# Where split weights are kept between chunks, and a new order at the start of a two-layer trunk

## The chip, the cores and the metric

The kernel runs on one NeuronCore of one Trainium2 chip. The metric is the device time in microseconds (us) of one execution, as the median of several runs. Beside the timed runs stands one profiled execution, from which every instruction's start and duration is known. In its rows PE is TensorE (PEld its weight loads), DVE is VectorE, ACT is ScalarE, POOL is GpSimd, and SP is SyncE, whose queue issues nearly all DMAs in order. A small q (SPq) marks an engine's sequencer.

## The reference, cut to what matters

The input x has 2048 tokens of 1024 channels. Layer A is a pooling mixer, layer B an attention whose weights are products of "keep" factors along the keys. Each layer ends with a gated embedding term.

```python
def rms_norm(x, g):
    return (x * lax.rsqrt(jnp.mean(x * x, axis=-1, keepdims=True) + EPS)) * g
...
for i in range(2):                                   # layer 0 is A, layer 1 is B
    if i == 0:                                       # A: pooling mixer
        h = rms_norm(x, a_norm[0])
        u, z = split(h @ w_in)                       # 1024 -> 2 x 1024
        pooled = trailing_mean(u, (2, 4, 8, 16)) - u # four groups of 256 channels
        mixed = einsum(pooled, w_group) * scale      # one 256 x 256 map a group
        x = x + (mixed * silu(z)) @ w_out
    else:                                            # B: stick-breaking attention
        k, v = split(rms_norm(x, kv_norm) @ w_kv)    # 16 heads of 64
        q, z = split(rms_norm(x, b_norm[0]) @ w_in)
        o = stick_breaking_attention(rms_norm(q), rms_norm(k), v)
        x = x + (o * silu(z)) @ w_out
    x = x + (p[i] @ ple_w[i]) * sigmoid(x @ ple_gate_w[i])
```

All of it is in float32.

## The kernel before

**Splitting.** A matrix operand is held as a pair: a high part, which is the number rounded to the type that TensorE takes at full rate (`float32r`), and a low part, the rest. A product of two pairs takes three matmuls: high by high, high by low, low by high. So each 128 x 512 piece of a weight, 0.26 MB as float32, becomes a pair of 0.52 MB. `put_split` (L145) makes it: one instruction on ACT rounds, one on POOL or DVE subtracts. Where a norm's gain belongs to the weight, ACT and DVE multiply by it on the way (L153, L154); where none does, two subtractions in three go to POOL and one to DVE (L147, L149).

**The plan of weights.** The list `plan` (L220 to L241) names every weight unit in the order in which TensorE takes it. `pump` (L179) loads units ahead of use, as many as `UNITS` = 9 weight tiles allow; a tile is given back (L191) when its last matmul is written. A unit with `keep` set is stored to scratch memory in HBM as a pair when it has been split (L169), and the next time its key comes up the pair is loaded as it is (L161). A unit without it is loaded raw (L164) into one of four `io` tiles, and split each time. The `io` tiles also serve the residual `xr`, the embedding input and the next chunk's x. Before, z of A (`za`), z of B (`zb`), and q, k, v are kept; the output weights `ao`, the gate `ag` and the embedding weights `al` of layer A are not.

**Stages.** The tokens are cut into four chunks of 512. For each chunk, `first_part` runs the mixer, the output projection (`out_steps`), the gate (`gate_steps`), z of B (`gate_z`), and q, k, v for the first eight heads (`kvq`, b = 0). `second_part` runs q, k, v for the other eight (b = 1). In chunk 0 each group's u weights are first multiplied with the group's map on the chip (`fold`), and the results kept as `wf`. A last pass, `post`, runs the output projection and gate of layer B for each chunk.

**Two streams on TensorE.** Chunk 0's first part runs alone, with six PSUM banks for dense products. From then on attention is written out slot by slot (L912 to L934), a slot being one head and one block of 512 keys, and `fill` puts a share of the dense stream's matmuls between the parts of each slot. There the dense products have two PSUM banks. `fill` also calls `keep` (L759) every 36 steps once the first half of chunk 1 is done: it loads one unit of layer B's output or gate weights, splits it, and stores it, 36 units in all.

**Order.** The order on each engine is chosen by a scheduler from the order written and its own estimate of times. With `state["hold"]` set, matmuls stay in the order written (L52); with `state["boot"]` set, so do the instructions passed through `booted`. At the start, `boot` (L395) loads the first weights and x, folds group 3 and computes the tokens' mean squares on TensorE (`sum_first`, L384): eight squares on ACT, and for each four products with a column of ones, which are two instructions each.

Of the kernel before, what the change touches and what calls it, by code (L numbers as in the profile page):

```python
# [11 lines left out]
AF = mybir.ActivationFunctionType  # L12
# [3 lines left out]
P = 128  # L16
D = 1024
S = 2048
KT = D // P
# [17 lines left out]
def trunk_kernel(ctx, tc, x, p, a_norm, wu_t, wz_a, w_group, a_scale, a_w_out, kv_norm, w_kv,  # L37
# [73 lines left out]
    def bank(tag, nm):  # L111
        return psum.tile([P, W5], F32, tag=tag, name=nm)
# [7 lines left out]
    def turned():  # L120
        return bank("psa", "pst").rearrange("q (j t) -> q j t", j=4)
# [7 lines left out]
    def booted(ins):  # L129
        if state["boot"]:  # L130
            tc.keep_in_program_order(ins)
# [47 lines left out]
    def pump():  # L179
        while wq["out"] < len(plan) and wq["out"] - wq["back"] < wq["cap"]:  # L180
            key, src, kts, n, gain, keep = plan[wq["out"]]
            if src is None and (key not in once or wq["out"] < first_chunk):
                return
            held.append(unit(key, src, kts, n, gain, keep))
            wq["out"] += 1

    def take(n):
        pump()
        return [held.popleft() for _ in range(n)]
# [7 lines left out]
    def plan_block(nm, src, b, gain=None, keep=False, order=PAIRS):  # L197
        for kts in order:
            plan.append(((nm, b, kts), None if src is None else src[b], kts, WB, gain, keep))

    def plan_wide(nm, src, b, gain):
        for kt in range(KT):
            plan.append(((nm, b, kt), src[b], (kt,), W5, gain, True))

    def plan_kvq(b):
        plan_wide("q", b_w_q, b, g_b)
        plan_wide("k", w_kv, b, g_kv)
        plan_wide("v", w_kv, 2 + b, g_kv)

    def plan_group(g):  # L210
        plan.append((("wg", g), w_group[g], (0, 1), WB, None, False))
# [8 lines left out]
    for s in range(NSUB):  # L220
        for g in (3, 2, 1, 0):
            if s == 0:
                plan_group(g)
            plan_block("za", wz_a, g, g_a, True)
            plan_block("wf", None, g)
        for b in range(4):
            plan_block("ao", a_w_out, b, order=PAIRS[::-1])
        for b in range(4):
            plan_block("ag", gate_a, b)
            plan_block("al", ple_a, b, order=PAIRS[:1])  # L230
        if s + 1 == NSUB:
            plan_kvq(0)
        for b in range(4):
            plan_block("zb", b_w_z, b, g_b, True)
        if s + 1 < NSUB:
            plan_kvq(0)
        plan_kvq(1)
        if s == 0:
            first_chunk = len(plan)
    for c in range(NSUB):  # L240
# [83 lines left out]
    def bcast(r, nm):  # L324
        ps = turned()
        for j in range(4):
            T.transpose(ps[:, j, :], r[:, j : j + 1].to_broadcast([P, P]), ident)
        rb = pool.tile([P, W5], F32, tag="rb", name="rb" + nm, bufs=2)
        A.copy(out=rb, in_=ps.rearrange("q j t -> q (j t)"))
        return rb  # L330
# [7 lines left out]
    def rooted(ps, nm):  # L338
        ss = pool.tile([P, 4], F32, tag="ss" + nm, name="ss")
        A.copy(out=ss, in_=ps[:, 0, 0:4])  # L340
        r = pool.tile([P, 4], F32, tag="r" + nm, name="r")
        rsqrt_mean(r, ss, D, nm)
        return r
# [14 lines left out]
    def load_first():  # L358
        two = [t4("u0") for _ in range(2)]
        for h in range(2):  # L360
            for c in range(2):
                first_u[c, h] = f(two[h])[:, c]
                ins = (nc.scalar if c else nc.sync).dma_start(out=first_u[c, h],
                                                             in_=wu_t[6 + c, :, h * W5 : (h + 1) * W5])
                if not c:
                    booted(ins)
            if h == 0:
                pump()
        nc.scalar.dma_start(out=g_a, in_=a_norm)
        for o in range(KT):  # L370
            xin = (qryt, ppt, keyt, valt)[(0, 2, 0, 3, 0, 2, 0, 3)[o]]("xin", F32)
            ins = (nc.scalar if o == 1 else nc.sync).dma_start(out=xin, in_=x[o * P : (o + 1) * P, 0:W5])
            if o != 1:
                booted(ins)
            first_x.append(xin)
# [5 lines left out]
            booted((G if o % 2 else V).tensor_tensor(out=pr[:, 1], in0=first_x[o], in1=f(pr[:, 0]), op=ALU.subtract))  # L381
            chunk[0].setdefault("x", []).append(pr)

    def sum_first():  # L384
        sums = turned()
        for i in range(KT):
            sq = tmp("sq")
            booted(A.activation(out=sq, in_=first_x[i], func=AF.Square))
            for j in range(4):
                tc.keep_in_program_order(  # L390
                    T.matmul(sums[:, 0, j : j + 1], sq[:, j * P : (j + 1) * P], ones,
                             start=(i + j == 0), stop=(i == KT - 1 and j == 3)))
        chunk[0]["rb1"] = bcast(rooted(sums, "x"), "x")

    def boot():  # L395
        load_first()
        later.pop(0)()
        fold_split(3, first_u)
        wq["cap"] = UNITS
        pump()  # L400
        run = fold(3)

        def folds(n):
            for _ in range(n):
                next(run, None)

        cast_first(range(4))
        folds(13)
        cast_first(range(4, KT))
        folds(12)  # L410
        later.pop(0)()
        folds(12)
        later.pop(0)()
        later.pop(0)()
        folds(12)
        later.pop(0)()
        sum_first()
        while later:
            later.pop(0)()
        for dst, v in ((g_s, a_scale), (g_b, b_norm), (g_kv, kv_norm), (gs[:, 0:1], k_norm), (gs[:, 1:2], b_q_norm)):  # L420
            nc.sync.dma_start(out=dst, in_=v)
        booted(V.scalar_tensor_tensor(out=gqk, in0=gs[:, 1:2], scalar=HD ** -0.5, in1=gs[:, 0:1],
                                      op0=ALU.mult, op1=ALU.mult))
        state["boot"] = False
        pump()

    def prep(s):
        ck = chunk[s]
# [23 lines left out]
    def pooled(s, o, ps, zr):  # L452
# [22 lines left out]
        split(pr, po, G if o > 1 else V)  # L475
        ck["m"][o] = pr

    def mixer(s):
        ck = chunk[s]
        ck["m"] = {}  # L480
        for g in (3, 2, 1, 0):
            if s == 0 and g < 3:
                yield from fold(g)
            us, zs = take(4), []
            for k in range(2):
                ps = dense()
                yield from product(ps, us, ck["x"], k * P, k)
                zs.append(silu(ps, ck["rb1"]))
            if s == 0 and g:
                fold_load(g - 1)  # L490
            us = take(4)
            for k in range(2):
                ps = dense()
                yield from product(ps, us, ck["x"], k * P, k)
                pooled(s, 2 * g + k, ps, zs[k])
# [405 lines left out]
    def fill(share):  # L901
        nonlocal owed, count
        owed += share
        while owed >= 1.0:
            next(run, None)
            owed -= 1.0
            count += 1
            if count % 36 == 0 and kept and (1, 0) in marks:
                keep(*kept.pop(0))

    scan = None
# [92 lines left out]
```

## Time and profile before

| | us |
|---|---|
| median of 3 runs (2810.36 to 2812.27) | 2812.25 |
| the profiled execution | 2817.46 |
| its span, first to last instruction | 2815.7 |
| PE busy | 2733.7 |
| DVE busy | 1847.9 |
| ACT busy | 1272.0 |
| POOL busy | 863.9 |

The DMA queues moved 643.37 MB at a mean of 228 GB/s over the span. The mean granted clock of TensorE was 0.985 of full.

How to read the rows that follow. A row of the waits gives who waited for whom, the total in us, how often, and the longest. A row of the busy times by stretch starts with the stretch in us from the span's start and its length, then each engine's busy time with the number of instructions in brackets (PE, PEld, DVE, ACT, POOL), then TensorE's granted clock, the share of the time in which the DMA engines were busy, and the GB/s that they moved. A row of the timeline gives start, duration, engine, line, operation, output and inputs, shape, the count of instructions merged into it, and in square brackets the idle time before it and what ended that. A row for one line or tile gives the count, the shortest, median and longest duration in ns, and the first and last start in us.

### The profile page before, as it was taken

The numbers are of one execution on the slowest core, as the hardware profiler recorded it, in microseconds if no ns is written. First come the engines' busy times: TensorE is split into PE (matmuls) and PEld (weight loads), VectorE is DVE, ScalarE is ACT, GpSimd is POOL, SyncE is SP. The second block draws the span as 40 slices with busy tenths as digits, with TensorE's granted clock in tenths as the row PEclk, the third lists the DMA queues.
The fourth block names the chain that finished last, engine by engine and source line by source line (L and its number), as shares of the span: only waits on it lengthen the run. The fifth ranks groups of instructions, "written<-read, shape, count | busy, mean of one in ns | idle before, by whom it ended". The sixth has DMA issues, their size and how long they took to land.

```text
span 2815.7 us, 38145 instructions
## 1 busy us (share of the span) xinstructions
PE 2733.7 (97%) x13400; PEld 2249.9 (80%) x13400; DVE 1847.9 (66%) x2373; ACT 1272.0 (45%) x2496; POOL 863.9 (31%) x695
## 2 busy tenths in 40 slices
PE   8999979999989999999999999999999999999999
PEld 7888857878867887788778888888888888888777
DVE  5745445755434786765558889777777877777872
ACT  5335543344334345544444456554554444444441
POOL 2354422445432354554222334221211101111002
PEclk9999989999999999999999999999999999999999
DMA  6648899556788966787785544778587767656545
GB/s 236 213 148 291 300 321 317 185 173 216 255 276 277 335 225 211 239 305 234 246 272 183 153 143 155 256 221 266 178 253 228 241 212 251 216 193 227 180 125 186
DMA packets 306123, 643.37 MB, mean 228 GB/s; under 512 B 48646, under 2 KB 81414, under 8 KB 305932
## 3 DMA queue, kind: packets, MB, share of 16 engines
q1 hardware_dynamic: 305356, 640.16, 68.9%
q8 instruction: 105, 1.72, 0.3%
q14 instruction: 86, 0.70, 0.1%
q10 hardware_dynamic: 576, 0.79, 0.1%
HBM read 471.43 MB, written 161.02 MB: 225 GB/s over the span
## 4 chain that ended last, share of the span: by engine, by line
PE 77%; DMA 9%; DVE 6%; issue 2%; SPq 2%; POOL 2%; ACT 2%; ACTq 0%; DVEq 0%; POOLq 0%
PE psd L46 53%; PE pso L46 8%; PE psl L46 8%; PE psa L50 7%; DMA wpair<-once 2%; DVE pp L815 2%; DMA vs<-vr 2%; DVE at L832 1%; DMA wraw<-in_gate_a_dram 1%; PE pst L50 1%; DMA wraw<-in_w_kv_dram 1%; DVE wpair L154 1%; DMA wraw<-in_b_w_q_dram 1%; PE pst L46 1%; SPq L595 0%
## 5 line engine op out<-in xcount | busy, mean ns | idle before, releaser
L815 DVE TENSOR_TENSOR_SCAN pp<-pp,floor 128x512 f32<-128x512 f32 (+3 forms) x640 | 777.0, 1214 | 26.4 <-ACT pp L811 25.5
L832 DVE TENSOR_TENSOR at<-psa,at 128x512 fp32r<-128x512 f32 (+3 forms) x640 | 387.1, 605 | 440.1 <-ACT at L830 437.7
L46 PE MATMUL psd<-wpair,x 128*128 128x512 f32 x2304 | 619.8, 403 | 33.6 <-DMA wpair<-once 17.1
L830 ACT CAST at<-psa 128x512 fp32r<-128x512 f32 (+3 forms) x640 | 333.4, 521 | 668.1 <-PE psa L50 644.5
L46 PE MATMUL psd<-x,wpair 128*128 128x512 f32 x2304 | 600.3, 393 | 2.1 <-ACT sg L546 2.1
L46 PEld LDWEIGHTS psd<-wpair,x 128*128 128x128 f32 x2304 | 427.7, 191 | 132.8 <-DMA wpair<-once 27.8
L46 PEld LDWEIGHTS psd<-x,wpair 128*128 128x128 f32 x2304 | 427.9, 188 | 91.0 <-ACT sg L546 2.8
L46 PE MATMUL psd<-xp,wpair 128*128 128x512 f32 x1536 | 390.0, 395 | 0.4 <-DMA wpair<-once 0.4
L46 PE MATMUL pso<-at,vv 128*128 128x512 f32 (+3 forms) x1280 | 362.4, 364 | 0.2 <-DVE at L832 0.2
L50 PE MATMUL psa<-ident,pp 128*128 128x128 f32 x2176 | 346.8, 274 | 14.2 <-DVE pp L815 5.7
L50 PEld LDWEIGHTS psa<-ident,pp 128*128 128x128 f32 x2176 | 274.6, 140 | 100.9 <-DVE at L832 11.1
L811 ACT ACTIVATE pp<-psl 128x512 f32<-128x512 f32 (+3 forms) x640 | 344.4, 538 | 6.6 <-PE psl L46 3.3
L46 PEld LDWEIGHTS psd<-xp,wpair 128*128 128x128 f32 x1536 | 286.6, 189 | 59.4 <-DMA wpair<-once 0.8
L46 PE MATMUL psl<-kk,qa 128*128 128x512 f32 (+3 forms) x640 | 284.4, 444 | 4.3 <-DMA kk<-kd 3.0
L46 PEld LDWEIGHTS pso<-at,vv 128*128 128x128 f32 x1280 | 241.8, 189 | 54.4 <-DVE at L832 0.5
L46 PE MATMUL psl<-kk,qb 128*128 128x512 f32 (+3 forms) x640 | 234.3, 366 | 0.0
L46 PE MATMUL psd<-mp,wpair 128*128 128x512 f32 x768 | 197.9, 399 | 6.9 <-DVE xr L514 6.9
L46 PE MATMUL psd<-og,wpair 128*128 128x512 f32 x744 | 202.5, 394 | 2.0 <-DVE os L845 2.0
L149 POOL TENSOR_TENSOR wpair<-wraw,wpair 128x512 fp32r<-128x512 f32 x101 | 146.8, 1458 | 138.1 <-ACT wpair L147 136.7
L46 PEld LDWEIGHTS psd<-mp,wpair 128*128 128x128 f32 x768 | 145.4, 192 | 38.1 <-DVE xr L514 7.7
L46 PEld LDWEIGHTS psd<-og,wpair 128*128 128x128 f32 x744 | 137.5, 188 | 31.3 <-DVE os L845 2.6
L539 POOL TENSOR_TENSOR xj<-x 128x512 f32<-128x512 f32 x64 | 101.8, 1594 | 134.2 <-DVE sg L550 127.5
(117 smaller groups left out, 2750.1 us busy)
## 6 DMA issues: line engine op xcount, KB each, us to landing
wpair<-once SPq DMA_DIRECT2D x384, 512.0 KB
once<-wpair SPq DMA_DIRECT2D x80, 512.0 KB
kk<-kd SPq DMA_DIRECT2D x160, 256.0 KB
vv<-vd SPq DMA_DIRECT2D x160, 256.0 KB
wpair<-wf SPq DMA_DIRECT2D x48, 512.0 KB
once<-kp SPq DMA_DIRECT2D x36, 512.0 KB
wraw<-in_a_w_out_dram SPq DMA_DIRECT2D x64, 256.0 KB
wraw<-in_gate_a_dram SPq DMA_DIRECT2D x64, 256.0 KB
```

Of the source, the lines that this page charges most:

```text
L46: return held_in_order(nc.tensor.matmul(*a, **k))
L50: return held_in_order(nc.tensor.transpose(*a, **k))
L149: (G if state["lo"] % 3 else V).tensor_tensor(out=pr[:, 1], in0=raw, in1=f(pr[:, 0]), op=ALU.subtract)
L154: booted(V.scalar_tensor_tensor(out=pr[:, 1, i], in0=raw[:, i], scalar=g, in1=f(pr[:, 0, i]), op0=ALU.mult, op1=ALU.subtract))
L539: G.tensor_tensor(out=xj, in0=f(x1[o][:, 0]), in1=f(x1[o][:, 1]), op=ALU.add)
L811: A.activation(out=pp[:, r0:], in_=ps[:, :w], func=AF.Sigmoid, scale=-1.0)
L815: V.tensor_tensor_scan(out=pp[:, r0:][:, ::-1], data0=pp[:, r0:][:, ::-1], data1=least, initial=1.0 if st["diag"] else st["carry"][j], op0 ...
L830: A.copy(out=at[:, 0, cs], in_=pt[:, cs])
L832: return lambda: V.tensor_tensor(out=at[:, 1, cs], in0=pt[:, cs], in1=f(at[:, 0, cs]), op=ALU.subtract)
```

## The change

It has four parts.

1. The units of q, k and v for the second eight heads (b = 1) are not stored in chunk 0. They are loaded raw again in chunk 1, split and stored there, and loaded as pairs in chunks 2 and 3.
2. The units of `ao`, `ag` and `al` (16, 16 and 4 a chunk) are stored as pairs in chunk 0 and loaded as pairs in chunks 1 to 3.
3. The start: matmuls are held in the written order from the first one on. Three matmuls of the identity with a constant tile, whose result nobody reads, are written ahead of the first fold. Then z's two products of group 3 come first, with the sums of the squares written between the matmuls of the second, then u's two products, with the norm's broadcast and z's SiLU written into the first. The loads of group 2's u weights are written behind them.
4. `keep` starts when the second half of chunk 1 is done, and runs every 54 steps in place of 36.

```diff
--- before.py
+++ after.py
@@ -198,14 +198,15 @@
         for kts in order:
             plan.append(((nm, b, kts), None if src is None else src[b], kts, WB, gain, keep))
 
-    def plan_wide(nm, src, b, gain):
+    def plan_wide(nm, src, b, gain, keep):
         for kt in range(KT):
-            plan.append(((nm, b, kt), src[b], (kt,), W5, gain, True))
-
-    def plan_kvq(b):
-        plan_wide("q", b_w_q, b, g_b)
-        plan_wide("k", w_kv, b, g_kv)
-        plan_wide("v", w_kv, 2 + b, g_kv)
+            plan.append(((nm, b, kt), src[b], (kt,), W5, gain, keep))
+
+    def plan_kvq(s, b):
+        keep = s >= b
+        plan_wide("q", b_w_q, b, g_b, keep)
+        plan_wide("k", w_kv, b, g_kv, keep)
+        plan_wide("v", w_kv, 2 + b, g_kv, keep)
 
     def plan_group(g):
         plan.append((("wg", g), w_group[g], (0, 1), WB, None, False))
@@ -224,17 +225,17 @@
             plan_block("za", wz_a, g, g_a, True)
             plan_block("wf", None, g)
         for b in range(4):
-            plan_block("ao", a_w_out, b, order=PAIRS[::-1])
+            plan_block("ao", a_w_out, b, keep=True, order=PAIRS[::-1])
         for b in range(4):
-            plan_block("ag", gate_a, b)
-            plan_block("al", ple_a, b, order=PAIRS[:1])
+            plan_block("ag", gate_a, b, keep=True)
+            plan_block("al", ple_a, b, keep=True, order=PAIRS[:1])
         if s + 1 == NSUB:
-            plan_kvq(0)
+            plan_kvq(s, 0)
         for b in range(4):
             plan_block("zb", b_w_z, b, g_b, True)
         if s + 1 < NSUB:
-            plan_kvq(0)
-        plan_kvq(1)
+            plan_kvq(s, 0)
+        plan_kvq(s, 1)
         if s == 0:
             first_chunk = len(plan)
     for c in range(NSUB):
@@ -381,19 +382,27 @@
             booted((G if o % 2 else V).tensor_tensor(out=pr[:, 1], in0=first_x[o], in1=f(pr[:, 0]), op=ALU.subtract))
             chunk[0].setdefault("x", []).append(pr)
 
-    def sum_first():
-        sums = turned()
-        for i in range(KT):
-            sq = tmp("sq")
-            booted(A.activation(out=sq, in_=first_x[i], func=AF.Square))
-            for j in range(4):
-                tc.keep_in_program_order(
-                    T.matmul(sums[:, 0, j : j + 1], sq[:, j * P : (j + 1) * P], ones,
-                             start=(i + j == 0), stop=(i == KT - 1 and j == 3)))
-        chunk[0]["rb1"] = bcast(rooted(sums, "x"), "x")
+    def square_first(i):
+        if i == 0:
+            chunk[0]["sums"] = turned()
+        sq = tmp("sq")
+        booted(A.activation(out=sq, in_=first_x[i], func=AF.Square))
+        for j in range(4):
+            T.matmul(chunk[0]["sums"][:, 0, j : j + 1], sq[:, j * P : (j + 1) * P], ones,
+                     start=(i + j == 0), stop=(i == KT - 1 and j == 3))
+
+    def norm_first():
+        chunk[0]["rb1"] = bcast(rooted(chunk[0].pop("sums"), "x"), "x")
+
+    def warm():
+        ps = bank("pso", "warm")
+        for _ in range(3):
+            T.matmul(ps, ident, floor, start=True, stop=True)
 
     def boot():
+        state["hold"] = True
         load_first()
+        warm()
         later.pop(0)()
         fold_split(3, first_u)
         wq["cap"] = UNITS
@@ -414,15 +423,10 @@
         later.pop(0)()
         folds(12)
         later.pop(0)()
-        sum_first()
-        while later:
-            later.pop(0)()
         for dst, v in ((g_s, a_scale), (g_b, b_norm), (g_kv, kv_norm), (gs[:, 0:1], k_norm), (gs[:, 1:2], b_q_norm)):
             nc.sync.dma_start(out=dst, in_=v)
         booted(V.scalar_tensor_tensor(out=gqk, in0=gs[:, 1:2], scalar=HD ** -0.5, in1=gs[:, 0:1],
                                       op0=ALU.mult, op1=ALU.mult))
-        state["boot"] = False
-        pump()
 
     def prep(s):
         ck = chunk[s]
@@ -475,11 +479,42 @@
         split(pr, po, G if o > 1 else V)
         ck["m"][o] = pr
 
+    def hooked(gen, hooks):
+        for n, _ in enumerate(gen):
+            for h in hooks.get(n, ()):
+                h()
+            yield
+
+    def mixer_first():
+        ck = chunk[0]
+        ck["m"] = {}
+        us = take(4)
+        pss = [dense(), dense()]
+        yield from product(pss[0], us, ck["x"], 0, 0)
+        hooks = {3 * i: [lambda i=i: square_first(i)] for i in range(KT)}
+        yield from hooked(product(pss[1], us, ck["x"], P, 1), hooks)
+        while later:
+            later.pop(0)()
+        us = take(4)
+        zs = []
+        hooks = {8: [norm_first], 9: [lambda: zs.extend(silu(ps, ck["rb1"]) for ps in pss)]}
+        for k in range(2):
+            ps = dense()
+            yield from hooked(product(ps, us, ck["x"], k * P, k), {} if k else hooks)
+            pooled(0, 6 + k, ps, zs[k])
+        state["boot"] = state["hold"] = False
+        fold_load(2)
+        while later:
+            later.pop(0)()
+
     def mixer(s):
         ck = chunk[s]
-        ck["m"] = {}
-        for g in (3, 2, 1, 0):
-            if s == 0 and g < 3:
+        if s == 0:
+            yield from mixer_first()
+        else:
+            ck["m"] = {}
+        for g in (3, 2, 1, 0)[s == 0 :]:
+            if s == 0:
                 yield from fold(g)
             us, zs = take(4), []
             for k in range(2):
@@ -905,7 +940,7 @@
             next(run, None)
             owed -= 1.0
             count += 1
-            if count % 36 == 0 and kept and (1, 0) in marks:
+            if count % 54 == 0 and kept and (1, 1) in marks:
                 keep(*kept.pop(0))
 
     scan = None
```

## The prediction

> **What bounds the kernel now.** I read the page first, then TensorE's waits, then the busy time and clock of each stage of chunk 0, then the instructions around the longest stalls.
>
> ```profile
> span 2815.7 us, 38145 instructions
> PE 2733.7 (97%) x13400; PEld 2249.9 (80%) x13400; DVE 1847.9 (66%) x2373; ACT 1272.0 (45%) x2496; POOL 863.9 (31%) x695
> once<-wpair SPq DMA_DIRECT2D x80, 512.0 KB
> PE psd L46 <- DMA wpair<-once: 17.5, 20, 4.8
> PE psd L46 <- ACT wpair L153: 14.0, 6, 9.3
> PE psd L46 <- ACT uh L293: 7.5, 2, 7.0
> PE psd L46 <- DVE xr L514: 6.9, 2, 4.1
> PE psd L46 <- ACT sg L546: 3.7, 3, 2.1
> PE psd L46 <- DMA wpair<-once: 14.8, 13, 4.8
> ```
>
> TensorE sets the time: it idles 82.0 us of 2815.7 (span less busy), and the change touches no matmul of the steady part. So all it can win is idle time and time at the halved clock. Nearly all named waits are late weights or late operands of dense products (the last line is the same view for 700 to 1000 us alone). The stages of chunk 0 (the columns behind the busy times are granted clock, DMA share, GB/s):
>
> ```profile
> 100.00:136.60 36.60, 36.60 (x186) 31.28 (x185) 24.14 (x40) 12.99 (x24) 16.16 (x16) 1.00 0.61 208
> 136.60:180.10 43.50, 43.50 (x194) 36.03 (x193) 18.46 (x25) 15.04 (x25) 20.31 (x16) 1.00 0.43 136
> 180.10:234.50 54.40, 54.40 (x242) 45.06 (x241) 36.23 (x45) 28.56 (x54) 31.17 (x22) 1.00 0.58 195
> 234.50:279.40 44.90, 44.90 (x206) 37.33 (x205) 21.66 (x33) 21.06 (x42) 17.13 (x14) 1.00 0.88 316
> 279.40:345.00 65.60, 65.60 (x301) 54.17 (x300) 31.48 (x44) 33.96 (x54) 32.00 (x29) 1.00 0.86 308
> 345.00:375.00 30.00, 15.79 (x60) 11.14 (x59) 8.66 (x13) 9.93 (x17) 5.51 (x5) 0.68 0.91 291
> 375.00:400.00 25.00, 23.47 (x98) 17.86 (x97) 11.19 (x17) 10.48 (x18) 7.85 (x9) 0.97 0.99 313
> 400.00:452.00 52.00, 49.03 (x226) 38.73 (x227) 26.68 (x40) 23.51 (x41) 12.47 (x11) 0.97 0.95 322
> 346.33 0.48 SPq L169 DMA_DIRECT2D once<-wpair  x1
> 369.04 0.43 SPq L169 DMA_DIRECT2D once<-wpair  x1
> ```
>
> In order these are the end of the mixer, A's output projection, gate, B's z, the first half's q/k/v, and (345 to 452) the second half's. The last three rows hold 14.2 + 1.5 + 3.0 = 18.7 us of idle TensorE at 291 to 322 GB/s and a DMA share over 0.9: here memory traffic is the bound. Seven stores of split weights are issued from the first to the second of the last two lines. Ahead of it, A's output projection uses 136 GB/s.
>
> **Step B, chunk 0's stores.** The 24 stores of the second half's q/k/v leave chunk 0; 16 + 16 + 4 = 36 stores of A's output, gate and embedding weights enter it. A store is 0.524 MB. Leaving: seven in 345 to 375, 3.67 MB, at that row's 291 GB/s 12.6 us of its 14.2 us idle. The other 17, 8.9 MB, are 36% of the 24.6 MB of the two rows behind, whose idle time of 4.5 us I take to vanish but for 0.5. Entering: 18.9 MB between about 111 and 234. At the 322 GB/s of the busiest row the spare room is 25.6 x 114 = 2.9 MB, 43.5 x 186 = 8.1 and 54.4 x 127 = 6.9, together 17.9 MB: 1.0 MB, or 3.1 us, is late, and the two rows behind have 1.2 MB of room for it. I take 10 us in 345 to 375, 4 us behind it, and 4 us of clock ((1 - clock) x busy gives at most 5.1 + 0.7 + 1.5 = 7.3): **-18**. Best: all 18.7 + 7.3, -26. Worst: the copies sustain only 308, the spare is 25.6 x 100 + 43.5 x 172 + 54.4 x 113 = 16.2 MB, 2.7 MB or 9 us is late and nothing behind absorbs it; with the q/k stores also part of the wait, -6. Each entering store waits at SP's head for its subtraction, and the next raw loads stand behind it; the lookahead of nine weight tiles hides that, and if it is used up, each late microsecond is TensorE's.
>
> A rule of the Trainium skill ("DMA: Bandwidth & Descriptors", Specifications) puts a core's HBM share near 358 GB/s, and its Bandwidth section has a single core alone at up to 425. No row of these stages passes 322 at a share of 0.95. With 358 the estimated lag is zero and B is 3 us better; the rows decide, so I keep 322.
>
> **Step C, output and gate of chunks 1 to 3.** The 36 units a chunk come back as one 0.5 MB load in place of a 0.25 MB load, a copy on ACT and a subtraction on POOL or DVE; 108 of each go. These run beside TensorE, so their busy time is worth nothing by itself. What counts is the four `io` tiles, which raw weights share with the residual `xr`:
>
> ```profile
> 566.00 6.44 SPq L508 DMA_DIRECT2D xr<-in_x_dram  x4
> 569.38 1.30 DVE L514 TENSOR_TENSOR xr<-psd,xr 128x512 f32<-128x512 f32 x2 [1.43 <-DMA xr<-in_x_dram]
> 570.12 4.61 PE L46 MATMUL psd<-mp,wpair 128*128 128x512 f32 x12 [2.78 <-DVE xr L514]
> 1059.81 1.65 PE L46 MATMUL psd<-mp,wpair 128*128 128x512 f32 x3 [4.07 <-DVE xr L514]
> 1618.91 0.47 PE L50 MATMUL psa<-ident,pp 128*128 128x128 f32 x1 [2.04 <-DVE pp L815]
> 550.00:600.00 50.00, 47.22 (x213) 38.30 (x212) 29.77 (x37) 21.38 (x43) 25.51 (x18) 0.97 0.51 162
> 1050.00:1100.00 50.00, 45.93 (x212) 37.69 (x212) 30.95 (x36) 22.91 (x47) 22.25 (x16) 0.93 0.61 200
> ```
>
> `xr` is loaded only behind raw weights, DVE adds it late, and the two PSUM banks hold TensorE. The xr waits are 6.9 us; sg's 3.7 and the 2.0 at 1618.91 stand behind queues that hold splits. The clock costs about 0.03 x 47 + 0.07 x 46 = 4.6 us more in the two stages. Of these 17.2 us I take **-10**: the pair loads too queue on SP ahead of xr, waiting for a weight tile. Bounds -17 (all) and 0 (none). The extra 9.4 MB a chunk go where DMA is at 162 to 200 GB/s.
>
> **Step D, the moved stores and `keep`.** Chunk 1's second half (about 820 to 920 us) now loads 0.25 MB raw, splits it and stores: 24 x 0.26 MB more traffic, 24 x (0.721 + 0.746) us on ACT and DVE. B's output weights, 36 units of 0.79 MB, start only after it, one per 54 steps for 36. Today's take 832.8 to 1226.0, 10.9 us each: about eight fewer lie there, 6.3 MB against 6.3 MB. At 10.9 x 1.5 = 16.4 us each, 36 of them from about 920 then reach to about 1510.
>
> ```profile
> L153 ACT ACTIVATE wpair<-wraw,gains x80: 493/721/728, 217.2 to 429.3; 128x512 fp32r<-128x512 f32 x48, 128x256 fp32r<-128x256 f32 x32
> L154 DVE SCALAR_TENSOR_TENSOR wpair<-wraw,gains,wpair x80: 471/746/1751, 218.1 to 430.0; 128x512 fp32r<-128x512 f32 x48, 128x256 fp32r<-128x256 f32 x32
> L149 POOL TENSOR_TENSOR kp<-kraw,kp x22: 1261/1294/2272, 832.8 to 1226.0; 128x512 fp32r<-128x512 f32 x22
> 800.00:850.00 50.00, 42.89 (x182) 34.19 (x181) 16.56 (x24) 15.60 (x30) 11.69 (x11) 0.90 0.95 304
> 850.00:900.00 50.00, 44.13 (x206) 34.73 (x205) 21.95 (x33) 20.21 (x40) 15.54 (x15) 0.93 0.79 272
> 1450.00:1500.00 50.00, 46.76 (x232) 38.58 (x233) 36.18 (x47) 21.76 (x46) 13.09 (x10) 0.97 0.90 282
> ```
>
> The new wait is the split's: behind ACT's copy stand the attention's sigmoids, behind DVE's subtraction the scans. DVE has room (22 of 50 us), so I take +1 there; bounds: -8 (half the weight bytes it waits for), +8 (half of L153's 14.0 plus clock). Past 1226 a keep per 16.4 us adds 48 GB/s, to 330 where the last row has 282 and idles 3.2 us in 50; the row at 304 idles 7.1. Over the 284 us I take +5, bounds 0 and +12 (three such stretches at 3.9 us more). **+6**.
>
> **Step A, the start.**
>
> ```profile
> 7.02 0.79 PE L46 MATMUL psd<-wpair,uh 128*128 128x256 f32 x2 [7.02 <-ACT uh L293]
> 16.72 12.88 PE L46 MATMUL psd<-xp,wpair 128*128 128x512 f32 x56
> 23.50 0.88 DVE L154 SCALAR_TENSOR_TENSOR wpair<-wraw,g_a,wpair 128x256 fp32r<-128x256 f32 x2
> 29.40:31.64 2.24, 2.24 (x22) 2.20 (x21) 0.00 (x0) 1.41 (x3) 0.95 (x1) 1.00 1.00 324
> 31.64:40.90 9.26, 9.26 (x45) 9.26 (x46) 3.17 (x7) 3.38 (x8) 0.32 (x1) 0.50 0.82 292
> 40.90:45.29 4.39, 4.39 (x11) 3.49 (x12) 1.55 (x3) 2.08 (x6) 1.24 (x2) 0.50 0.38 123
> 52.63 0.28 PE L46 MATMUL psd<-wpair,uh 128*128 128x256 f32 x1
> 58.38 21.95 PE L46 MATMUL psd<-xp,wpair 128*128 128x512 f32 x96
> ```
>
> Now TensorE starts at 7.02, does group 3's u products before z (the 56 at 16.72, while z's weights are still being split), then the squares' sums, and reaches the next fold at 52.63. After, three idle matmuls fill the wait before 7.02. No row has a full-precision 512-column matmul; at half rate a product takes 0.40 us (4.39/11), so three cost 1.2 us, or 4.8 at four passes, and either fits before 7.02: I take nothing. The fold then ends sooner, but the held order puts z first, and z's last weight is split only at 24.4: ACT and DVE work through a written order that a faster TensorE doesn't move. From there: z's last unit 6 x 0.229 (21.95/96) = 1.4, then 72 products, 16.5, the 64 instructions of sums at 0.102 (2.24/22), 6.5, and the broadcast 0.6: 49.4, 3.2 us sooner. The next u weights are now loaded behind the products: +1, near the 0.5 us that the second of L293's two waits cost (7.5 less 7.0). **-2**; best -5, worst the rival below.
>
> The idle matmuls are not the gain: the Trainium skill ("TensorE: Matmul & The Clock Gate", the part on the HAM clock gate) gives full rate after about 3.4 us of activity and half again after an idle window as long; the trace has it half 2.2 us into the sums, at 31.64. By the page the early clock is lost again while TensorE waits for z, and the estimate stays.
>
> **Sum.** -18 - 10 + 6 - 2 = -24 us on the profiled execution's 2817.46 (span 2815.7 and 1.8 around it): 2793.5. That execution is 5.2 us above the median of 2812.25; carried over, **2788 us**.
>
> **Rivals.** (1) The start goes cold: one-column sums do not count as activity (1.00 falls to 0.50 within 2.2 us at 31.64), and with sums between every three products only 0.69 of 1.51 us is dense. Then sums cost 0.206 (9.26/45) and products 0.40 (4.39/11): 64 x 0.104 + 24 x 0.17 = 10.7, so A is +9: 2799. For: the row; against: nearly half remains dense. (2) The 36 stores saturate chunk 0: B is -6: 2800. For: 17.9 MB of room for 18.9; against: the relief lies right behind. (3) Slower: pair loads wait at SP's head for a free weight tile and stall output and gate of chunks 1 to 3 as `once` does in 700 to 1000, 14.8 us on 48 q/k/v units, 0.31 us each. On 108 units +33 in place of -10: 2831. It decides from 0.13 us a unit, where it eats the other terms' 14. Against: DMA is at 162 to 200 there, not 304. (4) The stalls only move: 345 to 452 is held by the q/k/v traffic itself and xr by SP's order; B -6, C 0, D +6, A -2: 2810, no change.
>
> **Numbers.** Forecast 0.50, (1) 0.15, (2) 0.12, (3) 0.10, (4) 0.13. Faster by over 0.2% (5.6 us, about what this kernel's measurement tells apart): forecast, (1) and (2), 0.77; same 0.13; slower 0.10. Range: down, B's and C's best ends with the rest as taken, -39, 2773, and a little of D's, 2768; up to 2812, which takes in (1), (2) and (4) and leaves (3) and the far low end out. The forecast's own range, one term at a bound at a time: 2780 (B at -26) to 2800 (B at -6).
>
> **What would show it.** B: clock 1.00 and no wait on L153 at 345 to 452; over 300 GB/s at 136 to 234 without idle. C: no wait on xr in chunks 1 to 3, no raw casts behind 250 us but q/k/v's 24 and the keeps. D: idle at 1254 to 1500 above today's. A: first fold of group 2 near 50. It is wrong if TensorE stalls in 136 to 345, or if output and gate wait on `once`.

## The result, and the profile after

The changed kernel takes 2786.98 us (median of 4 runs, 2782.59 to 2787.66) against 2812.26 us of the kernel before (median of 4 beside it). The ratio is 0.9907 with a 95% interval of 0.9893 to 0.9921, a gain of 25.3 us. The profiled execution of the changed kernel has a span of 2785.8 us, 29.9 less than that of before. In the code after, the scan is L850, A's output projection adds `xr` in L549, and the gate's sigmoid is L581.

TensorE's waits after, the longest first (who waited for whom, us in total, times, longest):

```profile
PE psd L46 <- ACT wpair L153: 17.6, 4, 11.0
PE psl L46 <- DMA kk<-kd: 12.2, 2, 6.6
PE psd L46 <- DMA wpair<-once: 9.2, 13, 1.6
...
PE psd L46 <- ACT uh L294: 0.8, 1, 0.8
...
PE psd L46 <- ACT sg L581: 0.6, 1, 0.6
```

The wait on `xr` is gone and the one on the gate's sigmoid nearly so. Waits on stored pairs (`once`) have halved. But splits (L153) are waited for longer than before, 17.6 us against 14.0 (3.1 of them for z at the start), and a wait for the attention's keys, 3.0 us before, is now 12.2. The change moved waits as well as removing them. Where, the busy time by stretch shows, first in chunk 0, over the same stretches as in the prediction:

```profile
136.60:180.10 43.50, 43.50 (x194) 36.02 (x193) 13.13 (x17) 13.08 (x22) 18.07 (x14) 1.00 0.81 285
180.10:234.50 54.40, 53.32 (x235) 43.59 (x234) 36.13 (x47) 28.47 (x55) 31.93 (x22) 1.00 0.96 342
234.50:279.40 44.90, 44.90 (x206) 37.33 (x205) 21.97 (x34) 22.60 (x44) 18.89 (x15) 1.00 0.94 345
345.00:375.00 30.00, 21.08 (x86) 15.86 (x86) 12.75 (x19) 13.15 (x23) 10.88 (x10) 0.86 0.86 232
400.00:452.00 52.00, 51.88 (x253) 42.87 (x252) 23.63 (x36) 20.73 (x38) 9.44 (x9) 1.00 0.86 261
```

The 36 new stores are issued from 116.5 to 216.4: nine ahead of these rows, 13 in the first and 14 in the second. The first three rows have 285, 342 and 345 GB/s where it was 136, 195 and 316, and TensorE idles 1.1 us in all. In the fourth the traffic fell from 291 to 232 GB/s, the idle time from 14.2 to 8.9 us.

For the whole kernel I took from both traces the time between the first dense matmuls of successive stages:

| stage | before, us | after, us | change |
|---|---|---|---|
| start and mixer, chunk 0 | 136.6 | 131.7 | -4.9 |
| output, gate, z, chunk 0 | 142.8 | 144.4 | +1.6 |
| q, k, v (both halves), chunk 0 | 173.1 | 158.2 | -14.9 |
| mixer, chunk 1 | 101.6 | 101.4 | -0.2 |
| output, gate, z, chunk 1 | 171.6 | 165.6 | -6.0 |
| q, k, v, chunk 1 | 191.2 | 189.1 | -2.1 |
| mixer, chunk 2 | 124.1 | 124.9 | +0.8 |
| output, gate, z, chunk 2 | 212.5 | 201.1 | -11.4 |
| q, k, v, chunk 2 | 202.4 | 210.6 | +8.2 |
| mixer, chunk 3 | 157.0 | 161.8 | +4.8 |
| output and gate, chunk 3 | 175.2 | 170.4 | -4.8 |
| all that follows | 1027.6 | 1026.6 | -1.0 |

The stages with the largest changes in chunks 1 to 3 (output projection of chunk 1, its q/k/v, the same two of chunk 2, mixer of chunk 3), first before, then after:

```profile
554.10:609.30 55.20, 52.42 (x238) 42.70 (x237) 30.40 (x38) 22.02 (x45) 24.88 (x19) 0.97 0.50 161
725.70:916.90 191.20, 175.53 (x815) 140.36 (x814) 81.33 (x115) 77.49 (x153) 64.07 (x58) 0.96 0.81 269
1041.00:1109.20 68.20, 64.13 (x302) 52.71 (x301) 45.59 (x55) 32.03 (x65) 31.39 (x22) 0.95 0.63 205
1253.50:1455.90 202.40, 197.51 (x986) 161.07 (x985) 116.18 (x155) 93.99 (x185) 60.32 (x53) 0.99 0.76 244
1455.90:1612.90 157.00, 153.99 (x774) 127.19 (x773) 128.17 (x160) 71.78 (x144) 51.11 (x40) 0.99 0.61 191
```

```profile
535.70:586.00 50.30, 50.30 (x239) 41.77 (x238) 22.04 (x31) 12.92 (x28) 9.53 (x8) 1.00 0.79 258
701.30:890.40 189.10, 172.25 (x816) 140.64 (x815) 95.57 (x136) 89.81 (x172) 60.02 (x54) 0.95 0.84 277
1015.30:1076.40 61.10, 61.10 (x302) 50.60 (x301) 37.16 (x49) 22.73 (x49) 14.70 (x11) 1.00 0.82 268
1216.40:1427.00 210.60, 199.97 (x985) 161.91 (x984) 123.18 (x158) 98.41 (x193) 69.28 (x60) 0.98 0.80 265
1427.00:1588.80 161.80, 155.16 (x774) 128.12 (x773) 126.19 (x163) 71.91 (x146) 52.27 (x40) 0.97 0.72 237
```

The output projections run without a gap. The q/k/v stages of chunks 1 and 2 idle 16.9 and 10.6 us, before 15.7 and 4.9. In chunk 1 two waits on split weights, 14.2 us, stand where waits on stored pairs stood; the longest of all, from the timeline:

```profile
802.52 2.50 PE L46 MATMUL psd<-wpair,x 128*128 128x512 f32 x5 [10.98 <-ACT wpair L153]
795.41 0.34 SPq L169 DMA_DIRECT2D once<-wpair  x1
795.80 1.80 SPq L164 DMA_DIRECT2D wraw<-in_b_w_q_dram  x3
801.74 0.72 ACT L153 ACTIVATE wpair<-wraw,gains 128x512 fp32r<-128x512 f32 x1 [2.35 <-DMA wraw<-in_b_w_q_dram]
```

Three raw loads leave SP only right behind a store, at 795.8; ACT has the data at 801.7, TensorE its weight at 802.5.

### The profile page after: what moved, and what is told of

Same layout as the page of the kernel before. It is cut to its first block, busy times and chain, and to the rows that moved or that the text cites. A ratio compares the mean times of both kernels' runs of the same rounds, so it can differ in the third digit from the quotient of the medians.

```text
span 2785.8 us, 37906 instructions
## 1 busy us (share of the span) xinstructions
PE 2715.9 (97%) x13406; PEld 2238.1 (80%) x13406; DVE 1805.6 (65%) x2361; ACT 1229.2 (44%) x2412; POOL 754.1 (27%) x623
## 4 chain that ended last, share of the span: by engine, by line
PE 85%; DMA 7%; DVE 3%; SPq 2%; ACT 1%; issue 1%; POOL 1%; ACTq 0%; DVEq 0%; POOLq 0%
PE psd L46 59%; PE psl L46 8%; PE pso L46 8%; PE psa L50 8%; DMA wpair<-once 2%; DVE pp L850 2%; PE pst L50 1%; DVE at L867 1%; DMA wraw<-in_b_w_q_dram 1%; DMA vs<-vr 1%; DMA once<-kp 0%; DMA wraw<-in_gate_a_dram 0%; PE pst L46 0%; DMA xin<-in_x_dram 0%; DMA wraw<-in_w_kv_dram 0%
## 5 line engine op out<-in xcount | busy, mean ns | idle before, releaser
L850 DVE TENSOR_TENSOR_SCAN pp<-pp,floor 128x512 f32<-128x512 f32 (+3 forms) x640 | 762.2, 1191 | 33.7 <-ACT pp L846 32.0
L46 PE MATMUL psd<-wpair,x 128*128 128x512 f32 x2304 | 615.1, 402 | 25.2 <-ACT wpair L153 14.5
L846 ACT ACTIVATE pp<-psl 128x512 f32<-128x512 f32 (+3 forms) x640 | 344.4, 538 | 12.3 <-PE psl L46 8.2
L46 PE MATMUL psl<-kk,qa 128*128 128x512 f32 (+3 forms) x640 | 284.0, 444 | 12.2 <-DMA kk<-kd 12.2
L135 POOL TENSOR_TENSOR x<-xr,x 128x512 fp32r<-128x512 f32 x32 | 45.3, 1419 | 343.8 <-ACT x L134 343.8
L46 PEld LDWEIGHTS psl<-kk,qa 128*128 128x128 f32 x640 | 122.3, 191 | 18.3 <-ACT at L865 7.0
```

The lines of the kernel that those rows point to most:

```text
L46: return held_in_order(nc.tensor.matmul(*a, **k))
L135: lo.tensor_tensor(out=pr[:, 1], in0=src, in1=f(pr[:, 0]), op=ALU.subtract)
L846: A.activation(out=pp[:, r0:], in_=ps[:, :w], func=AF.Sigmoid, scale=-1.0)
L850: V.tensor_tensor_scan(out=pp[:, r0:][:, ::-1], data0=pp[:, r0:][:, ::-1], data1=least, initial=1.0 if st["diag"] else st["carry"][j], op0 ...
```

## The experiments

All were timed in three rounds beside the kernel before, whose medians in the four later sets of runs were 2809.4 to 2811.8. Times compare to the changed kernel's 2787.0 and its interval of 0.9893 to 0.9921.

### Each part undone

**Part 1 undone.**

```diff
-        keep = s >= b
+        keep = True
```

> The changed kernel with part 1 undone: the second half's q, k, v are stored in chunk 0 again, beside the 36 stores of layer A's weights. Theory (step B, stores leaving): the products of q, k, v in chunk 0, which the change shortened by 14.9 us by the two traces, lose that again, and the 36 stores ahead of them now find no relief behind: 2802 to 2812 us. Chunk 1's second half loads pairs again, between 0 and -3 us. Rival (the wait at 345 to 452 is the q/k/v traffic itself, and the stores' place does not matter): at most 2792.

Measured: 2797.5 us, ratio 0.995 (0.9935 to 0.9966). The mixer of chunk 1 starts at 447.9 against 434.3, so chunk 0 lost 13.6 of the 14.9 us: the place of these stores matters, as step B has it. The longest waits of chunk 0's q/k/v:

```profile
PE psd L46 <- ACT wpair L153: 14.5, 6, 8.9
PE psd L46 <- DVE wpair L154: 2.1, 2, 1.5
```

The time grew by 10.6 only, below the stated 15 to 25. The profiled execution, with a span 15.6 us longer, was the slowest of its four, so 13.6 may be high. Chunk 1's q/k/v was 3.0 us shorter (186.1), as the expectation allowed, but runs alike there differ by more (185.0 to 189.3). The rival, at most 2792, is out.

What no run separates is how the stores hold the raw loads up: by their bytes, or by standing before them in SP's queue. For the bytes: in 340 to 376 of the profile before, where the wait of 9.3 us lies, SP itself waited 0.3 us. For the queue: in 300 to 400 it waited 12.3 us for the subtractions of pairs that it was to store.

**Part 2 undone.**

```diff
-            plan_block("ao", a_w_out, b, keep=True, order=PAIRS[::-1])
+            plan_block("ao", a_w_out, b, order=PAIRS[::-1])
```

and the same for `ag` and `al`.

> The changed kernel with part 2 undone: A's output, gate and embedding weights are loaded raw and split in every chunk. Theory (step C, the io tiles hold back xr): output and gate of chunks 1 to 3, which the change shortened by 22.3 us by the two traces, lose all of it, chunk 0's output and gate win back 1.7: about 2807 us, with waits on xr of 5 us or more back in the waits. Rival (it was the place of keep, or the order in SP's queue, that shortened them): at most 2797, no xr waits.

Measured: 2801.9 us, ratio 0.9966 (0.9955 to 0.9978), 14.9 us slower than with it, where about 20 was stated. Output, gate and z (output and gate in chunk 3) of chunks 1 to 3 take 169.8, 210.7 and 175.2 us, 18.6 more than in the changed kernel. The mixer of chunk 1 starts 3.6 us earlier than there. The waits in chunk 2's stage came back, though more of them on the gate's sigmoid than on `xr`:

```profile
PE psd L46 <- ACT sg L581: 6.0, 2, 3.5
PE psd L46 <- DVE xr L549: 1.9, 1, 1.9
```

So part 2 is worth some 15 us net. That xr alone would hold 5 us or more was wrong (4.2 in all).

**Part 3 undone.** The start as it was; parts 1, 2 and 4 as changed.

```diff
     def boot():
-        state["hold"] = True
         load_first()
-        warm()
...
         later.pop(0)()
+        sum_first()
+        while later:
+            later.pop(0)()
...
+        state["boot"] = False
+        pump()
```

> The changed kernel with part 3 undone: the start as it was, parts 1, 2 and 4 as changed. Theory: the output projection of chunk 0 starts 4.9 us later and nothing behind absorbs it: 2790 to 2793 us. Rival (chunk 0 is bound by its DMAs from 111 us on, so that an earlier start only waits there): 2785 to 2788.

Measured: 2789.9 us, ratio 0.9918 (0.9903 to 0.9933). The intervals overlap, so the time does not tell. The trace does: chunk 0's output projection starts at 132.4 us, and the mixer of chunk 1 at 434.1, in the changed kernel at 131.7 and 434.3. The order of the start earned 0.7 us, and the stages up to the mixer of chunk 1 took even that back. The other 4.2 of the 4.9 us in the table are no effect of the change: with the same old start, runs differ in how long TensorE's clock is halved during the sums. The stretch 28 to 48 us of two of them, the kernel before, and the one further down with `xr` in another pool:

```profile
28.00:48.00 20.00, 20.00 (x94) 18.32 (x93) 6.05 (x12) 7.41 (x16) 2.50 (x3) 0.66 0.75 259
```

```profile
28.00:48.00 20.00, 20.00 (x110) 17.94 (x109) 7.93 (x15) 10.54 (x20) 3.47 (x4) 0.83 0.81 278
```

In four runs with this start (before, this one, parts 1 and 2 alone, `xr` in another pool) the clock over this stretch is 0.66, 0.74, 0.74 and 0.83, TensorE does 94, 103, 103 and 110 matmuls in it, and the output projection starts at 136.6, 132.4, 133.3 and 131.2. The profiled execution of before was the slowest of the four. In the ten profiles with the new start, it starts at 131.1 to 132.8.

**Part 4 undone.**

```diff
-            if count % 54 == 0 and kept and (1, 1) in marks:
+            if count % 36 == 0 and kept and (1, 0) in marks:
```

> The changed kernel with part 4 undone: the splitting of layer B's weights starts after chunk 1's first half, every 36 steps. Theory (step D): q, k, v of chunk 2 and the mixer of chunk 3, which the change made 13.0 us longer by the two traces, win that back; chunk 1's second half has 6.3 MB more and loses about 8: 2780 to 2785 us, part 4 by itself costs time. Rival (chunk 1's second half with its 24 new stores cannot bear the keeps beside it): qkv of chunk 1 at least 15 us longer, 2790 us or more.

Measured: 2781.0 us, ratio 0.9895 (0.9878 to 0.9912). By stage: q/k/v of chunk 1 takes 196.7 us, 7.6 more; q/k/v of chunk 2 and the mixer of chunk 3 take 201.3 and 159.3, 11.8 less. Both are what the theory stated, and the rival's 15 us more in chunk 1 did not come. The intervals overlap, so it is the traces rather than the time that say part 4 costs: with the late keeps, chunk 2's q/k/v takes 210.6 to 213.3 us in six profiles, and 201.3 to 202.7 in the six others that store all of q, k and v.

### The parts alone, and single causes

**Parts 1 and 2 alone** (the kernel before with part 1's and part 2's lines).

```diff
+        keep = s >= b
...
+            plan_block("ao", a_w_out, b, keep=True, order=PAIRS[::-1])
```

> The kernel before with parts 1 and 2 alone: the start and keep as before. Theory after the first four runs (parts 1 and 2 carry all of the gain, part 3 nothing that lasts, part 4 costs some 6 us): 2780 to 2785 us, no slower than the changed kernel. Rival (the parts need each other, as each was seen only with the other three in place): 2790 or more.

Measured: 2783.4 us, ratio 0.99 (0.9882 to 0.9918). The two parts carry the whole gain; the start and the later `keep` add nothing to it.

**No idle matmuls.**

```diff
         load_first()
-        warm()
         later.pop(0)()
```

> The changed kernel without the three idle matmuls. Theory (step A: ACT's and DVE's order sets when z's weights are there, and TensorE waits for them whatever its clock): the first z product starts within 0.5 us of 17.6, group 2's fold within 1 us of 39.8, the time within 2 us of the changed kernel's 2787. Rival (the early clock is worth the half rate it saves): the fold of group 2 starts 2 to 4 us later, and so does the end.

Measured: 2785.9 us, ratio 0.9918 (0.9903 to 0.9933). The first z product starts at 17.2, group 2's fold at 38.8 and the output projection at 131.5, against 17.6, 39.8 and 131.7 with them. (Of the fold, these are its first six matmuls; the others come behind u's products.) The idle matmuls are worth nothing. The changed kernel's start shows why. From its timeline, the idle matmuls; then by stretch, the empty time while z's weights are being split, the first z products, and the time of the sums:

```profile
1.83 4.28 PE L46 MATMUL warm<-floor,ident 128*128 128x512 f32 x6 [1.83 <-POOL floor L64]
```

```profile
14.50:17.50 3.00, 0.00 (x0) 0.00 (x0) 2.12 (x4) 2.08 (x6) 2.83 (x2) 1.00 0.80 276
18.40:21.80 3.40, 3.40 (x9) 2.30 (x8) 2.86 (x8) 2.43 (x6) 0.00 (x0) 0.50 1.00 400
25.20:37.10 11.90, 11.90 (x86) 10.95 (x84) 2.57 (x6) 5.53 (x12) 1.28 (x1) 1.00 0.83 277
```

TensorE waits 3.1 us for z, and the clock is halved right behind that wait, from 18.4 to 21.8; all nine profiles with the idle matmuls have some half clock there. Without the idle matmuls group 3's fold ends 1.0 us later, the wait is 1.7 us, and the clock stays at full:

```profile
18.40:21.80 3.40, 2.89 (x13) 1.94 (x12) 2.49 (x7) 2.76 (x7) 0.00 (x0) 1.00 1.01 405
```

So what the early clock gains is lost again behind the longer wait.

**xr in another pool**, in the kernel before.

```diff
-                xr = io("xr")
+                xr = tmp("xr")
```

> The kernel before with one change: the residual xr is loaded into a tile of another pool (six buffers), not into one of the four io tiles that the raw weights use. Theory (step C, xr waits for an io tile): the xr waits of 6.9 us go, output of chunk 1 and 2 become 5 to 7 us shorter each, 2800 to 2806 us. Rival (xr is late by its place in SP's queue behind raw loads that wait): xr waits of 4 us or more stay, 2808 to 2812.

Measured: 2798.6 us, ratio 0.9965 (0.9952 to 0.9978), faster than expected, but not where expected. TensorE's waits on `xr` fell to 3.7 us, between the two theories:

```profile
PE psd L46 <- DVE xr L514: 3.7, 2, 2.4
```

The output of chunks 1 and 2 became 3.1 and 2.9 us shorter (52.1 and 65.3), not 5 to 7. The start became 5.3 us shorter, which the paragraph on part 3 explains, and chunk 0's q/k/v 5.6 us, with no `xr` in it; why stays open. So the `io` tiles are about half of why TensorE waited for `xr`. The other half goes with the raw weights, as no such wait is left where pairs are loaded.

**keep in chunk 3.**

```diff
-            if count % 54 == 0 and kept and (1, 1) in marks:
+            if count % 36 == 0 and kept and (2, 1) in marks:
```

> The changed kernel with keep from the end of chunk 2's second half on, every 36 steps, so that it falls on chunk 3, whose rows hold 180 to 265 GB/s. Theory (step D: the keeps cost by the traffic they add where q, k, v already take 250 to 310 GB/s): q, k, v of chunk 2 and the mixer of chunk 3, 210.6 and 161.8 us in the changed kernel, fall back to about 202 and 157: 2771 to 2778 us. Rival (a keep costs wherever it runs, by its split on ACT, POOL and DVE): 2784 to 2790, the loss only moves into chunk 3.

Measured: 2777.9 us, ratio 0.989 (0.9876 to 0.9905), 9 us better than the changed kernel; its interval overlaps by 0.0012. In its trace q/k/v of chunk 2 is back at 201.7 us, and the mixer of chunk 3, which now has the keeps, at 160.5. The q/k/v stage of chunk 2 before, with late keeps (after) and without (this run) moves 244, 265 and 239 GB/s; this run's row:

```profile
1211.20:1412.90 201.70, 196.92 (x986) 161.12 (x985) 115.44 (x155) 92.64 (x182) 58.50 (x53) 0.99 0.75 239
```

The keeps are not free in chunk 3: its output and gate take 173.7 us against 170.4 in the changed kernel, and all that follows 1028.5 against 1026.6. But that is 5 us, where chunk 2's q/k/v alone lost 8.9. Of the rest of the gain, 4.1 us are in chunk 1's q/k/v (185.0), which the edit does not touch: they lie within its scatter (185.0 to 189.3 in runs alike there).

**A's pairs stored but not used.** The 36 stores of chunk 0 are made; chunks 1 to 3 load raw.

```diff
-        if key in once:
+        if key in once and key[0] not in ("ao", "ag", "al"):
             nc.sync.dma_start(out=f(pr), in_=once[key])
```

(and each pair is stored the first time only).

> The changed kernel with the 36 stores of layer A's weights made in chunk 0, but the pairs never loaded: chunks 1 to 3 load raw and split, as in the run with part 2 undone (2802 us). Theory (step B, stores entering): chunk 0 stays as in the changed kernel, q, k, v of chunk 0 from about 276 and the next mixer at 434 against 430.7 without the stores, so they cost 3 to 4 us: 2803 to 2808. Rival (they cost nothing, the 3.6 us are one run's scatter): 2800 to 2803, next mixer at 432 or before.

Measured: 2805.4 us, ratio 0.9982 (0.9969 to 0.9995). The mixer of chunk 1 starts at 433.8, with the stores in the changed kernel at 434.3, without them at 430.7. That is 3 us by three traces; the times, 2805.4 and 2801.9, have overlapping intervals and don't settle it alone. In the seven other runs that make these stores and the same q/k/v stores in chunk 0, it starts at 432.8 to 436.2. So the stores cost 2 to 5 us, measured against the one trace without them.

**keep in chunk 3, and xr in the other pool.**

```diff
-                xr = io("xr")
+                xr = tmp("xr")
...
-            if count % 54 == 0 and kept and (1, 1) in marks:
+            if count % 36 == 0 and kept and (2, 1) in marks:
```

> The kernel with keep in chunk 3 (2778 us), and xr loaded into the other pool. Theory (with pairs in chunks 1 to 3 nothing holds xr back any more, so the io tiles were the whole of it): no change, 2775 to 2781. Rival (xr in the io tiles also holds back the raw loads of chunk 0 and the keeps): 2768 to 2773, with q, k, v of chunk 0 shorter.

Measured: 2773.2 us, ratio 0.986 (0.9834 to 0.9886), against 0.9876 to 0.9905 without the second edit: not told apart. The spans are 2775.3 and 2775.6 us, neither trace has a wait of TensorE on `xr`, and chunk 0's q/k/v, which the rival had shorter, is not (159.3 against 156.7). With pairs in chunks 1 to 3, xr holds nothing back.

### The moved stores

**Second half never stored**, on the kernel with keep in chunk 3.

```diff
-        keep = s >= b
+        keep = b == 0
```

> The kernel with keep in chunk 3 (2778 us), and the second half's q, k, v never stored: raw and split in all four chunks. Theory (the 12.1 us that chunk 1's q, k, v wait for split weights come from the 24 stores moved there, which share the copies and SP's queue): that wait falls to 3 us or less, q, k, v of chunk 1 from 185 to some 176 us; chunks 2 and 3 move 6.3 MB less each and pay 24 splits: 2767 to 2774 us. Rival (it comes from loading raw at all: io tiles and split behind attention's work on ACT and DVE): the wait stays at 8 us or more in chunk 1 and appears in chunks 2 and 3: 2780 to 2795.

Measured: 2759.1 us, ratio 0.9817 (0.9797 to 0.9836), better than stated, and the fastest kernel here: 52 us faster than before, 28 faster than the changed kernel. In chunk 1 q/k/v took 172.6 us in place of 185.0. TensorE's waits there, with the stores and without them:

```profile
PE psd L46 <- ACT wpair L153: 12.1, 2, 8.3
PE psd L46 <- DMA wpair<-once: 1.8, 4, 1.0
```

```profile
PE psd L46 <- ACT wpair L153: 2.7, 1, 2.7
PE psd L46 <- DMA wpair<-once: 1.9, 4, 1.0
```

So the wait on splits that the change brought into chunk 1 comes from the 24 stores, not from loading raw. Whether it is their bytes or their place in SP's queue, this run does not separate either. Chunk 2's q/k/v got 4.2 us shorter too (197.5), though it now splits 24 units more on ACT and DVE.

**No q, k, v stored.**

```diff
-        keep = b == 0
+        keep = False
```

> The run before last's fastest kernel (2759 us: keep in chunk 3, second half of q, k, v raw in every chunk) with the first half raw in every chunk too, so that no q, k, v weight is stored. Theory (a pair's load and its store cost more on the copies than the split costs on ACT and DVE, as long as these have room): 12.6 MB of stores leave chunk 0's busiest rows, the 6.4 us that the first attention slot waits for its keys fall by half or more, chunks 1 to 3 move 6.3 MB less each: 2745 to 2755 us. Rival (ACT, DVE or the four io tiles become the bound with 48 splits a chunk): waits on split weights of 10 us or more in chunks 1 to 3, 2762 us or more.

Measured: 2763.3 us, ratio 0.983 (0.9812 to 0.9847): not faster, and not told apart from the run above. The theory missed. The rival has the time, but not its sign: waits on split weights are 7.3 us in all, not 10 or more in chunks 1 to 3. Chunk 0 gained as stated (mixer of chunk 1 at 427.9 against 436.1, the first attention slot no longer waits for its keys). From there to the end it gave 13 us back, some 10 of them from chunk 3's mixer on. The longest waits of the whole run are on DVE as much as on split weights; the last row is the first one's in the run above:

```profile
PE psa L50 <- DVE at L867: 8.5, 14, 1.6
PE psd L46 <- ACT wpair L153: 7.3, 5, 3.1
PE pst L50 <- DVE qs L659: 7.2, 3, 3.1
```

```profile
PE psa L50 <- DVE at L867: 3.8, 7, 1.2
```

The run above has no wait on `qs`. DVE's busy time is 1888.4 us here and 1836.6 with the first half stored. But that the added subtractions hold up what stands behind them in DVE's queue is not shown: ahead of the three waits on `qs`, DVE itself was idle, waiting for POOL's `rq`. The longest of them:

```profile
730.36 1.74 DVE L659 TENSOR_TENSOR qs<-qs,rq 128x512 f32<-128x512 f32 x1 [1.32 <-POOL rq L127]
```

Why these waits come up when no unit is stored stays open.

## Why the prediction was right, and where its steps were not

The time came out 1 us from the forecast, and the sum of -24 met a measured -25.3. Its terms were less exact than that.

**B, stores of chunk 0: -18 predicted, -13.3 by the traces (+1.6 and -14.9).** Right in kind: undoing part 1 alone brought 13.6 us back. The whole q/k/v stage of chunk 0, before and after:

```profile
279.40:452.50 173.10, 154.40 (x684) 122.31 (x683) 78.01 (x113) 77.89 (x129) 57.83 (x53) 0.93 0.92 310
276.10:434.30 158.20, 149.28 (x683) 121.80 (x683) 77.47 (x113) 78.21 (x129) 58.17 (x52) 0.97 0.81 258
```

It lost 9.8 us of idle time, where I had taken 14, and 5.1 us of busy time, where I had taken 4 for the clock. I let 4.2 us of 14.2 remain in 345 to 375; 8.9 remained, as a new wait took the place of the old, the first slot's keys (`kk<-kd`), 5.6 us. Rival 4 had warned of the q/k/v traffic itself.

The ceiling of 322 GB/s was wrong as well: the copies took 342 to 345 over 99 us. I had taken it from the stages behind 100 us alone. The start of the same profile has more:

```profile
16.70:29.40 12.70, 12.70 (x58) 10.54 (x57) 6.12 (x16) 8.47 (x19) 1.38 (x1) 1.00 0.92 350
```

I took the 3.1 us of late stores to be absorbed behind; some 3 us stayed, and not for the stated reason: at 345 GB/s the room would have been 20.8 MB, enough for all 18.9. Why 3 us stay is open. The Trainium skill's 358 ("DMA: Bandwidth & Descriptors", Specifications) was nearer for this mix, but it is no limit here: the 400 GB/s at 18.4 to 21.8 lie above it. SP had issued only stores of pairs since 15.4:

```profile
18.45 0.32 SPq L169 DMA_DIRECT2D once<-wpair  x1
19.87 0.32 SPq L320 DMA_DIRECT2D wf<-wpair  x1
20.67 1.18 SPq L169 DMA_DIRECT2D once<-wpair  x2
```

It was a mistake to read the largest rate of some stages as the largest there is.

**C, output and gate: -10 predicted, -22.2 by the traces, 18.6 by undoing it.** The step that failed is "the pair loads too queue on SP ahead of xr": no wait of TensorE on `xr` is left. The traces split the 22.2 into 12.8 us of idle time and 9.4 us of busy time for the same matmuls, whose clock was 0.95 to 1.00 before and is 1.00 after. I had at most 12.6 and 4.6, so the bound of -17 was too narrow by the clock; 2.0 of the 9.4 are chunk 3's, which I had not charged. And by the run with `xr` in another pool, the four `io` tiles were only about half of the cause of the waits on it.

**D, moved stores and keep: +6 predicted, +11.7 by the traces** (-2.1, +0.8, +8.2, +4.8). The collision of the late keeps with chunk 2's q/k/v was named and priced at 5; it was 13, of which 11.8 come back with the old cadence. The +1 for chunk 1's second half hid two larger numbers: waits on stored pairs fell, and 14.2 us on splits came. In the kernel with keep in chunk 3, the stage is 12.4 us shorter without the stores.

**A, the start: -2 predicted, -4.9 by the traces, 0.7 by undoing it.** The working held: z's products ended at 25.2 against the 25.8 worked out, u's at 49.8 against 49.4, and the idle matmuls gained nothing. What failed is the 52.6 of before, from which I subtracted. It was one execution's, with its scatter of the clock. The fold of group 2, first in the changed kernel behind u's products, then with the old start:

```profile
49.79 0.28 PE L46 MATMUL psd<-wpair,uh 128*128 128x256 f32 x1
```

```profile
49.50 0.28 PE L46 MATMUL psd<-wpair,uh 128*128 128x256 f32 x1
```

In the two other runs with the old start it begins at 50.0 and 48.5. The new order is no sooner there. The Trainium skill's rule on the clock gate ("TensorE: Matmul & The Clock Gate", the part on the HAM clock gate) agrees with the trace in kind: half rate again behind the wait for z (18.4 to 21.8), though that wait, 3.1 us, is a little shorter than the page's window.

**The rivals.** (1) did not come: with sums between the products the clock stayed at 1.00 (the stretch 25.2 to 37.1). (2) did not come, for the reason under B. (3) did not come: no wait on `once` in output or gate. (4) came in part, in `kk<-kd`.

So the terms missed by +5, -12, +6 and -3, together -5. That is about what the profiled execution of before lay above its median, so the two medians differ by just what was forecast. The hit to a microsecond was luck. The range was earned by the bounds only in part: C lay outside its own, and the sum stayed inside as the misses cancelled.

## What to carry to other kernels

A stored pair costs two transfers of double size and saves a split. Here splitting again was cheaper for some of the units: never storing half of the q/k/v weights was 19 us faster than storing them in chunk 1, while doing so for all of them gained nothing more, with new waits on DVE's results. Where raw tiles held back other loads, as in output and gate, storing pairs paid. Before you subtract from a milestone of one profile, see how far it scatters over several. And look at what a moved transfer lands on: the same 36 keeps cost some 12 us between chunk 2's q/k/v and chunk 3's mixer, 8 in chunk 1 and 5 in chunk 3.

## What was not expected of the hardware

The granted clock is halved in the same instructions for a different time from run to run: 0.66 to 0.83 over 28 to 48 us, worth up to 5 us at the start of one profile. The copies reached 345 GB/s with loads and stores mixed and 400 with stores of pairs alone, where the stage rows of before had at most 322 behind 100 us. One-column matmuls alone were followed by the half clock (before, 31.6 to 40.9), though weight loads ran all the time (9.26 of 9.26 us). Mixed among 512-column matmuls, three of these per eight, they were not: 86 matmuls in 11.9 us at 1.00.
